# The first norm of a hybrid encoder step: x fetched transposed, with the factor per token spread by a matmul of ones

## The chip, the cores and the metric

The kernel runs on one core of a Trainium2 chip. A time is device microseconds (us) of one execution; the time of a kernel is the median of its runs. The engines are TensorE (PE, whose weight loads are listed apart as PEld), VectorE (DVE), ScalarE (ACT), GpSimd (POOL) and SyncE (SP, which here only issues DMAs).

## The reference, cut to what matters

One layer of an encoder runs over 2048 prompt tokens and 128 sample tokens. What the change touches is the first line: the norm of x and the projection behind it.

```python
def rms_norm(x, g):
    xf = x.astype(jnp.float32)
    y = xf * lax.rsqrt(jnp.mean(xf * xf, axis=-1, keepdims=True) + EPS)
    return (y * g.astype(jnp.float32)).astype(x.dtype)

h = rms_norm(x, norm_g[0])          # x: tokens x 1024
z = h @ w_in                        # 1024 x 3592, columns split among head groups
# band attention (8 heads), mLSTM (4 heads), w_out, residual,
# then the gated FFN with a causal convolution of width 3, residual
```

## The kernel before

**Work and stages.** The 2176 tokens are 17 tiles of 128: tiles 0 to 15 of the prompt and tile 16, the sample (SAMPLE in the code). They go in two halves, each in chunks of three tiles: [0 1 2] [3 4 5] [6 7 16], then [8 9 10] [11 12 13] [14 15]. For each half the kernel runs 14 weight groups of w_in in a fixed order, va0, qk0, qk1, va1 and so on; every matmul product is made of three (helper `mm3`, L105 to L107), of a high and a low float32r part of each operand. PE needs the model dimension on the partitions, so that the normed rows of a tile, tokens on the partitions, have to be turned: eight 128x128 blocks for each tile, 136 in all.

**One tile of the norm** (`norm_tile`, called by `norm_steps`). SP fetches the tile's 512 KB of rows into `xr` (L225). ACT squares it with a sum per row (L229). POOL makes mean and power -0.5 (L88, L94). DVE multiplies rows by the factor and by norm's row g, which one DMA has spread over all partitions (L232, L99). PE turns the eight blocks into one PSUM tile of two banks, `hT_pt` (L77). ACT rounds that to the high part (L211), DVE subtracts for the low part (L212). The chunk tile `hT` that results is what the projections of all 14 groups read.

**Buffers.** `xr` has no buffer of its own: tiles 0, 3, 6 and 8 to 15 take one of two buffers of the tag "xr", tiles 1, 4, 7 and 16 that of attention's "pth", tiles 2 and 5 that of "ptl" (`xr_tag`). A tile's fetch therefore waits until an earlier tile has let its buffer go. PSUM tiles of the tag "big" have two buffers, shared with attention's scores. A weight group arrives in two raw halves (`wi_raw`, L1231, one buffer after another from a pool with one buffer), each split by ACT and DVE (L1237, L1238) into the high and low part.

**Order.** The kernel is written as generators whose steps are interleaved by estimated costs: `pump` advances the attention and mLSTM pipelines while their DVE cost lags 0.615 of the PE cost. The framework's scheduler then sets the order of each engine's own queue; each engine, and SP's DMA queue, works its queue strictly in that order and waits at the head of it. In the first half no attention is under way during group va0, so that its nine tiles of norm and its projections stand alone at the start; in the second half the norm of tiles 8 to 15 lies beside the last group of the first half and va0 of the second. At the start SP also carries the chain of the attention bias (`reln`, `ext`, `relrow`, `nb`).

Of the kernel before, what the change touches and what calls it, by code (L numbers as in the profile page):

```python
# [10 lines left out]
F32 = mybir.dt.float32  # L11
F32R = mybir.dt.float32r
AF = mybir.ActivationFunctionType
ALU = mybir.AluOpType
# [3 lines left out]
P = 128  # L18
# [32 lines left out]
def hymba_step(ctx: ExitStack, tc: tile.TileContext, I: dict, O: dict):  # L51
# [38 lines left out]
    def rsqrt_mean(ssq, n, name, eps=EPS):  # L90
        ms = small.tile([P, 1], F32, tag="ms", name=name + "_ms")
        mean_square(ms, ssq, n, eps)
        rs = small.tile([P, 1], F32, tag="rs", name=name + "_rs")
        nc.gpsimd.tensor_tensor(rs, ms, nhalf[:, 0:1], op=ALU.pow)  # L94
# [127 lines left out]
    def norm_tile(t, chunk, j, bank):  # L222
        tag = xr_tag(t)
        xr = rows_tile(tag, [P, D], f"xr{t}")
        nc.sync.dma_start(xr, x_src(t))  # L225
        if not g0:
            g0.append(norm_row(0))
        ssq = small.tile([P, 1], F32, tag="ssq", name=f"ssq{t}")
        nc.scalar.activation(chunk[:, 0, :, j * P:(j + 1) * P], xr.rearrange("p (k c) -> p k c", k=KT), AF.Square,  # L229
                             accum_out=ssq)  # L230
        rs = rsqrt_mean(ssq, D, f"n0_{t}")
        nc.vector.scalar_tensor_tensor(xr, xr, rs, g0[0], op0=ALU.mult, op1=ALU.mult)  # L232
        rows_to_T(xr, chunk, j, f"hT{t}", bank)

    def evac_scaled(out, in_, scale):
        if scale is None:
# [1006 lines left out]
    def norm_steps(half):  # L1243

        for ci, tiles in enumerate(HALVES[half]):
            ch = phT.tile([P, 2, KT, 384], F32R, tag="hT", name=f"hT{half}_{ci}", bufs=3)
            chunks.append(ch)
            for j, t in enumerate(tiles):
                norm_tile(t, ch, j, ps_big)
                yield 0.9, 2.5  # L1250

    seq = [(half, gi) for half in range(2) for gi in range(14)]
    g0 = []
    pipes += [Pipe(att_stream()), Pipe(mem_stream())]
    chunks = []
    norms = norm_steps(0)
# [2 lines left out]
    for _ in pend[2]:  # L1259
        pass  # L1260
    next(norms)
    load_bias()
    for n_, (half, gi) in enumerate(seq):
        wh, wl, _ = pend
        split = iter([])
        if n_ + 1 < len(seq):
            pend = load_group(seq[n_ + 1][1])
            split = pend[2]
        g = GROUPS[gi]
        i = int(g[2])  # L1270
        nm = f"{g}_{half}"
        if g[:2] == "va":
            it = group_rows(wh, wl, half, chunks, vd[i], nm, 264 if gi == 0 else 256,
                            [O["v_prompt"][i], O["v_sample"][i].unsqueeze(1)])
        elif g[:2] == "qk":
            it = group_T(wh, wl, half, chunks, [qTd[i], kTd[i]], [-(DA ** -0.5), None], nm,
                         [None, [O["k_prompt"][i], O["k_sample"][i]]])
        elif g[:2] == "qb":
            it = group_T(wh, wl, half, chunks, [[t_[:, c, :] for t_ in qkbd[i]] for c in range(2)],
                         [None, DH ** -0.5], nm)  # L1280
        else:
            it = group_rows(wh, wl, half, chunks, vobd[i], nm)
        if half == 0 and gi == 13:
            chunks = []
            norms = norm_steps(1)
        if n_ == len(seq) - 1:
# [621 lines left out]
def lay_inputs(inp):  # L1908
    import numpy as np

    c = np.ascontiguousarray
    w_in = inp["w_in"][0].reshape(KT, P, 3592).transpose(1, 0, 2)
    va = [w_in[:, :, 1024 + 256 * i:1280 + 256 * i] for i in range(2)]
    gt = w_in[:, :, 3584:3592]
    qk = [np.concatenate([w_in[:, :, P * i:P * i + P], w_in[:, :, 512 + P * i:640 + P * i]], 2) for i in range(4)]
    qb = [np.concatenate([w_in[:, :, 1536 + P * i:1664 + P * i], w_in[:, :, 2048 + P * i:2176 + P * i]], 2)
          for i in range(4)]
    vo = [np.concatenate([w_in[:, :, 2560 + P * i:2688 + P * i], w_in[:, :, 3072 + P * i:3200 + P * i]], 2)
          for i in range(4)]
# [7 lines left out]
    out = {  # L1927
        "x_prompt": inp["x_prompt"][0],
        "x_sample": inp["x_sample"].reshape(P, D),
        "norm_g": inp["norm_g"][0],  # L1930
        "g_att": inp["g_att"].reshape(4, P).transpose(1, 0),
        "g_mlstm": inp["g_mlstm"],
        "w_in0": np.concatenate([va[0], gt], 2).reshape(P, 2112),
        "w_in1": np.stack(rest).reshape(13, P, 2048),
        "b_gate": np.concatenate([inp["b_i"], inp["b_f"]], 1),
        "rel_rev": inp["rel_table"][0][:, ::-1],
        "w_out": inp["w_out"][0].reshape(KT, P, D).transpose(1, 0, 2).reshape(P, KT * D),
        "w_up": w_up.reshape(NF, P, 2048),
        "w_conv": wc.reshape(4, 44, P).transpose(2, 1, 0),
        "w_down": np.stack([w_dn[:, :, i, j] for i, j in ((0, 0), (0, 1), (1, 1), (1, 0))], 2).reshape(NK, P, 2048),  # L1940
        "cache_k": inp["cache_k_att"][0].reshape(DB, 4, 2, 512, DA).transpose(0, 1, 2, 4, 3).reshape(DB, 4, P, 512),
        "cache_v": inp["cache_v_att"][0].reshape(DB, HA, 4, P, DA).transpose(0, 3, 2, 1, 4).reshape(DB, P, 4, 512),
        "cache_conv": inp["cache_ffn_conv"][0].reshape(DB, 2, 44, P).transpose(3, 2, 0, 1),
        "state_c": np.concatenate([inp["state_mlstm_n"][0][..., None], inp["state_mlstm_c"][0]], 3).transpose(1, 2, 0, 3),
        "state_m": inp["state_mlstm_m"][0].transpose(1, 0),
    }
    return {k: c(v) for k, v in out.items()}
# [51 lines left out]
```

## Time and profile before

| what | value |
|---|---|
| median of three runs | 2747.54 us (2746.0 to 2754.83) |
| span of the profiled execution, first to last instruction | 2745.7 us |
| the median above this span | 1.8 us |
| PE busy | 97% of the span |
| DVE, ACT, POOL busy | 70%, 53%, 26% |
| DMA, mean over the span | 203 GB/s |

The profile is of one execution; the time around its span is the 1.8 us of the table when it is set against the median. Busy shares are means over stages with different limits: the first 60 us and the FFN that fills the second half have little in common, so a stage is read by its own window.

### The profile page before, as it was taken

The numbers are of one execution on the slowest core, as the hardware profiler recorded it, in microseconds if no ns is written. First come the engines' busy times: TensorE is split into PE (matmuls) and PEld (weight loads), VectorE is DVE, ScalarE is ACT, GpSimd is POOL, SyncE is SP. The second block draws the span as 40 slices with busy tenths as digits, with TensorE's granted clock in tenths as the row PEclk, the third lists the DMA queues.
The fourth block names the chain that finished last, engine by engine and source line by source line (L and its number), as shares of the span: only waits on it lengthen the run. The fifth ranks groups of instructions, "written<-read, shape, count | busy, mean of one in ns | idle before, by whom it ended". The sixth has DMA issues, their size and how long they took to land.

```text
span 2745.7 us, 47826 instructions
## 1 busy us (share of the span) xinstructions
PE 2672.3 (97%) x16323; PEld 2500.7 (91%) x16323; DVE 1922.9 (70%) x3643; ACT 1456.3 (53%) x2961; POOL 708.5 (26%) x1373
## 2 busy tenths in 40 slices
PE   7999999999999999999999999999999999999998
PEld 7899999998899998877899997789999888999976
DVE  5345445646546667756899998758888876899956
ACT  4355545635346666634445556654554665555554
POOL 1000010212100002335455542023333212565401
PEclk9999999999999999999999999999999999999999
DMA  5544355546564557668887668767886777798875
GB/s 184 159 118 139 106 156 166 170 151 206 156 192 125 154 157 225 195 213 287 300 244 229 219 203 271 246 198 200 223 221 189 230 252 239 212 246 240 254 260 184
DMA packets 335635, 557.03 MB, mean 203 GB/s; under 512 B 61890, under 2 KB 168222, under 8 KB 335070
## 3 DMA queue, kind: packets, MB, share of 16 engines
q1 hardware_dynamic: 253230, 406.60, 48.1%
q0 software_dynamic: 43568, 113.54, 14.3%
q10 hardware_dynamic: 38592, 33.83, 3.7%
q8 instruction: 128, 2.10, 0.3%
q14 instruction: 117, 0.96, 0.1%
HBM read 389.77 MB, written 173.49 MB: 205 GB/s over the span
## 4 chain that ended last, share of the span: by engine, by line
PE 42%; DVE 5%; DMA 3%; issue 1%; ACT 1%; POOL 0%; DVEq 0%; SPq 0%; POOLq 0%; ACTq 0%
PE uec L105 5%; PE uec L106 5%; PE uec L107 5%; PE dn L107 3%; PE dn L105 3%; PE dn L106 3%; PE ua L107 3%; PE ua L105 3%; PE ua L106 3%; PE ub L107 1%; PE ub L106 1%; PE ub L105 1%; PE dnm L107 1%; PE dnm L106 1%; PE dnm L105 1%
## 5 line engine op out<-in xcount | busy, mean ns | idle before, releaser
L105 PE MATMUL uec<-B,wuh 128*128 128x384 f32 (+1 forms) x720 | 236.0, 328 | 6.0 <-DVE ug L1498 3.8
L106 PE MATMUL uec<-B,wuh 128*128 128x384 f32 (+1 forms) x720 | 235.1, 327 | 0.0
L107 PE MATMUL uec<-B,wul 128*128 128x384 f32 (+1 forms) x720 | 234.4, 327 | 0.0
L1327 ACT CAST wuh<-wu 128x512 fp32r<-128x512 f32 x255 | 141.7, 618 | 110.9 <-PE uec L106 107.7
L1328 DVE TENSOR_TENSOR al<-ar,ah 128x768 fp32r<-128x768 f32 (+2 forms) x141 | 108.7, 780 | 117.4 <-ACT ah L1327 117.1
L107 PE MATMUL dn<-wdh,al 128*128 128x512 f32 x462 | 186.1, 403 | 3.6 <-DVE al L1328 3.6
L105 PE MATMUL dn<-wdh,ah 128*128 128x512 f32 x462 | 183.5, 397 | 4.6 <-ACT ah L1327 2.9
L106 PE MATMUL dn<-wdl,ah 128*128 128x512 f32 x462 | 182.6, 395 | 0.0
L1327 ACT CAST ah<-ar 128x768 fp32r<-128x768 f32 (+2 forms) x141 | 96.1, 692 | 151.3 <-PE dnm L106 113.3
L1328 DVE TENSOR_TENSOR wul<-wu,wuh 128x512 fp32r<-128x512 f32 x255 | 164.7, 686 | 2.4 <-ACT wuh L1327 2.4
L406 DVE CUSTOM_DVE_ANT_0 tmp<-s,nb 128x640 f32<-128x640 f32 (+4 forms) x128 | 94.4, 738 | 92.8 <-PE s L396 92.1
L105 PE MATMUL vo<-wi_h,hT 128*128 128x256 f32 x544 | 155.6, 286 | 0.6 <-DVE mt L212 0.6
L107 PE MATMUL vo<-wi_h,hT 128*128 128x256 f32 x544 | 155.9, 287 | 0.0
L106 PE MATMUL vo<-wi_l,hT 128*128 128x256 f32 x544 | 155.1, 285 | 0.0
L1328 DVE TENSOR_TENSOR wdl<-wdr,wdh 128x512 fp32r<-128x512 f32 x231 | 145.5, 686 | 8.0 <-ACT wdh L1327 5.9
L105 PEld LDWEIGHTS uec<-B,wuh 128*128 128x128 f32 x720 | 135.1, 188 | 9.1 <-issue 4.7
L106 PEld LDWEIGHTS uec<-B,wuh 128*128 128x128 f32 x720 | 135.3, 188 | 0.2
L105 PE MATMUL qk<-hT,wi_h 128*128 128x384 f32 (+1 forms) x384 | 129.1, 336 | 6.2 <-ACT qk_st L237 4.7
L107 PEld LDWEIGHTS uec<-B,wul 128*128 128x128 f32 x720 | 135.1, 188 | 0.0
L419 DVE TENSOR_TENSOR ptl<-pt,pth 128x640 fp32r<-128x640 f32 (+4 forms) x128 | 93.6, 738 | 57.9 <-ACT pth L418 57.0
L1327 ACT CAST wdh<-wdr 128x512 fp32r<-128x512 f32 x231 | 127.2, 620 | 11.6 <-PE uec L106 7.4
L407 ACT ACTIVATE tmp<-tmp,mn 128x640 f32<-128x640 f32 (+4 forms) x128 | 97.6, 763 | 64.7 <-DVE mn L406 61.9
(425 smaller groups left out, 9201.7 us busy)
## 6 DMA issues: line engine op xcount, KB each, us to landing
wu<-in_w_up SPq DMA_DIRECT2D x220, 256.0 KB, 4.4
wu<-wsd SPq DMA_DIRECT2D x176, 256.0 KB, 5.3
wdr<-wtd SPq DMA_DIRECT2D x132, 256.0 KB, 4.6
wi_raw<-in_w_in SPq DMA_DIRECT2D x52, 512.0 KB, 4.1
wdr<-in_w_down SPq DMA_DIRECT2D x99, 256.0 KB, 4.9
wsd<-ws POOLq DMA_DIRECT2D x88, 256.0 KB, 5.1
ar<-ad_S SPq DMA_DIRECT2D x50, 384.0 KB, 5.2
kraw<-kTd SPq DMA_DIRECT2D x112, 128.0 KB, 3.5
```

The lines of the kernel that those rows point to most:

```text
L105: nc.tensor.matmul(out, ah, bh, start=start, stop=False, skip_group_check=onto)
L106: nc.tensor.matmul(out, ah, bl, start=False, stop=False, skip_group_check=onto)
L107: nc.tensor.matmul(out, al, bh, start=False, stop=stop, skip_group_check=onto)
L406: nc.vector.tensor_tensor_reduce(o_, s_, b_, 1.0, 3e38, ALU.add, ALU.min, accum_out=mn)
L407: nc.scalar.activation(tmp[:, :n], tmp[:, :n], AF.Exp, bias=mn, scale=-1.0, accum_out=rsum[:, i % 4, hh:hh + 1])
L419: nc.vector.tensor_tensor(s.ptl[:, sl, qc], ptv, s.pth[:, sl, qc], op=ALU.subtract)
L1327: nc.scalar.copy(h, r)
L1328: nc.vector.tensor_tensor(l, r, h, op=ALU.subtract)
```

## The change

Each tile of x is now fetched twice. `x_T` is laid out by the host as the transposed tile, 1024 values on each of 128 partitions, partition by model dimension within a block of 128. `norm_factor` fetches the rows as before (`xq`), but only for the sum of squares; its power of -0.5 is written to one column of `nrs`. For tiles 0 to 7 and 16 it is called within the tile's step, for tiles 8 to 15 during groups 1 to 4 of the first half. `norm_tile` then works on the transposed tile `xt`: POOL multiplies it by g, which is now a column of eight values per partition (`g0`), spread along the tokens; POOL scales the identity by the tile's factors (`diag`); PE multiplies a matrix of ones by that, in float32, so that each partition of PSUM holds the 128 factors as a row; DVE multiplies `xt` by that row; ACT rounds and DVE subtracts, both from SBUF now. The steps announce 0.2 in place of 0.9 of PE cost to `pump`.

```diff
-        xr = rows_tile(tag, [P, D], f"xr{t}")
+    def norm_factor(t):
+        xr = rows_tile("xr", [P, D], f"xq{t}") if 8 <= t < SAMPLE else pa.tile(
+            [P, D], F32, tag=("kh", "kl")[t % 2], name=f"xq{t}", bufs=2)
         nc.sync.dma_start(xr, x_src(t))
-        if not g0:
-            g0.append(norm_row(0))
-        nc.scalar.activation(chunk[:, 0, :, j * P:(j + 1) * P], xr.rearrange("p (k c) -> p k c", k=KT), AF.Square,
-                             accum_out=ssq)
-        rs = rsqrt_mean(ssq, D, f"n0_{t}")
-        nc.vector.scalar_tensor_tensor(xr, xr, rs, g0[0], op0=ALU.mult, op1=ALU.mult)
-        rows_to_T(xr, chunk, j, f"hT{t}", bank)
+        nc.scalar.activation(xr, xr, AF.Square, accum_out=ssq)
+        mean_square(ms, ssq, D)
+        nc.gpsimd.tensor_tensor(nrs[:, t:t + 1], ms, nhalf[:, 0:1], op=ALU.pow)
+    def norm_tile(t, chunk, j):
+        xt = rows_tile(xr_tag(t), [P, D], f"xt{t}")
+        nc.sync.dma_start(xt, I["x_T"][t])
+        if not 8 <= t < SAMPLE:
+            norm_factor(t)
+        nc.gpsimd.tensor_tensor(xt, xt, g0.unsqueeze(2).broadcast_to([P, KT, P]), op=ALU.mult)
+        diag = pa.tile([P, 256], F32, tag="sh", name=f"diag{t}", bufs=1)[:, :P]
+        nc.gpsimd.tensor_scalar(diag, ident, nrs[:, t:t + 1], None, op0=ALU.mult)
+        row = ps_big(f"hT{t}_rs")[:, :P]
+        nc.tensor.matmul(row, ones, diag, start=True, stop=True)
+        nc.vector.tensor_tensor(xt, xt, row.unsqueeze(1).broadcast_to([P, KT, P]), op=ALU.mult)
+        nc.scalar.copy(chunk[:, 0, :, cols], xt)
+        nc.vector.tensor_tensor(chunk[:, 1, :, cols], xt, chunk[:, 0, :, cols], op=ALU.subtract)
...
-                norm_tile(t, ch, j, ps_big)
-                yield 0.9, 2.5
+                norm_tile(t, ch, j)
+                yield 0.2, 2.5
...
+            if half == 0 and 1 <= gi <= 4 and u % 6 == 3:
+                for t in [next(factors, None)]:
+                    if t is not None:
+                        norm_factor(t)
```

Three places of the queues bear on what follows. The first is SP's queue at the start, up to the second half of the first weight group, `wi0_raw1`; `xr`, `xt` and `xq` are the tiles of x with their numbers. Before, from the queue's first fetch:

```order
L225 DMA xr0_319<-in_x_prompt 128x1024
L99 DMA norm_row0_321<-in_norm_g 128x1024
L1231 DMA wi0_raw0_343<-in_w_in0 128x1056
L225 DMA xr1_355<-in_x_prompt 128x1024
L302 DMA reln_375<-in_rel_rev 8x384
L225 DMA xr2_394<-in_x_prompt 128x1024
L225 DMA xr3_446<-in_x_prompt 128x1024
L1304 DMA bgate_306<-in_b_gate 128x8
L1305 DMA gatt_317<-in_g_att 128x4
L616 DMA mss_885<-in_state_m 4x8
L504 DMA hgm0_0_4058<-in_g_mlstm 128x128
L1231 DMA wi0_raw1_349<-in_w_in0 128x1056
```

After, behind the queue's first seven fetches (g0, xt0, xq0, wi0_raw0, xt1, xq1, reln):

```order
L241 DMA xt2_391<-in_x_T 128x1024
L231 DMA xq2_393<-in_x_prompt 128x1024
L241 DMA xt3_440<-in_x_T 128x1024
L231 DMA xq3_442<-in_x_prompt 128x1024
L1329 DMA bgate_310<-in_b_gate 128x8
L231 DMA xq4_492<-in_x_prompt 128x1024
L1330 DMA gatt_321<-in_g_att 128x4
L636 DMA mss_913<-in_state_m 4x8
L524 DMA hgm0_0_4049<-in_g_mlstm 128x128
L99 DMA norm_row1_13054<-in_norm_g 128x1024
L1251 DMA wi0_raw1_349<-in_w_in0 128x1056
```

Of fetches of 512 KB and more, `wi0_raw1` was the seventh and is now the twelfth.

The second is the same queue further on, where the sample tile 16 is fetched, the last tile of the first half. Before, from the fourth fetch behind `wi0_raw1` on:

```order
L225 DMA xr4_499<-in_x_prompt 128x1024
L1231 DMA wi1_raw0_392<-in_w_in1 128x1024
L225 DMA xr5_550<-in_x_prompt 128x1024
L225 DMA xr7_651<-in_x_prompt 128x1024
L1231 DMA wi1_raw1_497<-in_w_in1 128x1024
L225 DMA xr8_6702<-in_x_prompt 128x1024
L1231 DMA wi2_raw0_812<-in_w_in1 128x1024
L225 DMA xr16_700<-in_x_sample 128x1024
```

After, behind `wi0_raw1`, ext, xq5, ext, xt6, xq6, xq7, xq16, xt4, relrow, xt5, wi1_raw0, xq8 and nb0 (in this order):

```order
L241 DMA xt7_633<-in_x_T 128x1024
L231 DMA xq9_1008<-in_x_prompt 128x1024
L335 DMA relrow_302<-ext_955 128x767
L335 DMA relrow_302<-ext_955 128x767
L1251 DMA wi1_raw1_488<-in_w_in1 128x1024
L231 DMA xq10_1184<-in_x_prompt 128x1024
L335 DMA relrow_302<-ext_955 128x767
L231 DMA xq11_1286<-in_x_prompt 128x1024
L358 DMA nb1_0_1366<-relrow_302 128x640
L241 DMA xt16_679<-in_x_T 128x1024
```

The transposed sample tile now stands behind the rows of tiles 9 to 11, the second half of the next weight group and four of the eight bias fetches, which stood behind it before. The buffer of xq9 is that of xt6, the buffer of xt7 that of xt4.

The third is POOL's queue for tiles 3 to 7 and 16. Before, it held two small instructions for each tile:

```order
L88 TENSOR_SCALAR n0_3_ms_450<-ssq3_448 128x1
L94 TENSOR_TENSOR n0_3_rs_452<-n0_3_ms_450,nhalf_77 128x1
L88 TENSOR_SCALAR n0_4_ms_503<-ssq4_501 128x1
L94 TENSOR_TENSOR n0_4_rs_505<-n0_4_ms_503,nhalf_77 128x1
L88 TENSOR_SCALAR n0_5_ms_554<-ssq5_552 128x1
L94 TENSOR_TENSOR n0_5_rs_556<-n0_5_ms_554,nhalf_77 128x1
```

After, from the product of tile 6 on:

```order
L245 TENSOR_TENSOR xt6_587<-xt6_587,g0_298 128x1024
L247 TENSOR_SCALAR diag5_548<-ident_72,nrs_299 128x128
L88 TENSOR_SCALAR n0_6_ms_593<-ssq6_591 128x1
L236 TENSOR_TENSOR nrs_299<-n0_6_ms_593,nhalf_77 128x1
L247 TENSOR_SCALAR diag6_597<-ident_72,nrs_299 128x128
L88 TENSOR_SCALAR n0_7_ms_639<-ssq7_637 128x1
L236 TENSOR_TENSOR nrs_299<-n0_7_ms_639,nhalf_77 128x1
L88 TENSOR_SCALAR n0_16_ms_685<-ssq16_683 128x1
L245 TENSOR_TENSOR xt4_490<-xt4_490,g0_298 128x1024
L236 TENSOR_TENSOR nrs_299<-n0_16_ms_685,nhalf_77 128x1
L245 TENSOR_TENSOR xt5_538<-xt5_538,g0_298 128x1024
L247 TENSOR_SCALAR diag7_643<-ident_72,nrs_299 128x128
```

A product of 128x1024 and a scaled identity have come in for each tile, and the products of tiles 4 and 5 stand behind that of tile 6 and behind the factors of tiles 6, 7 and 16.

More of the change, by code (lines that the diff above doesn't have):

```diff
@@ L220, in rows_tile @@
         return pa.tile(shape, dtype, tag=tag, name=name, bufs=1)
-    def norm_tile(t, chunk, j, bank):
-        tag = xr_tag(t)
-        xr = rows_tile(tag, [P, D], f"xr{t}")
+    g0 = const.tile([P, KT], F32, name="g0")
+    nrs = const.tile([P, 17], F32, name="nrs")
+    ones = pa.tile([P, P], F32, tag="ones", name="ones", bufs=1)
+    nc.vector.memset(ones, 1.0)
+    def norm_factor(t):
+        xr = rows_tile("xr", [P, D], f"xq{t}") if 8 <= t < SAMPLE else pa.tile(
+            [P, D], F32, tag=("kh", "kl")[t % 2], name=f"xq{t}", bufs=2)
         nc.sync.dma_start(xr, x_src(t))
-        if not g0:
-            g0.append(norm_row(0))
         ssq = small.tile([P, 1], F32, tag="ssq", name=f"ssq{t}")
-        nc.scalar.activation(chunk[:, 0, :, j * P:(j + 1) * P], xr.rearrange("p (k c) -> p k c", k=KT), AF.Square,
-                             accum_out=ssq)
-        rs = rsqrt_mean(ssq, D, f"n0_{t}")
-        nc.vector.scalar_tensor_tensor(xr, xr, rs, g0[0], op0=ALU.mult, op1=ALU.mult)
-        rows_to_T(xr, chunk, j, f"hT{t}", bank)
+        nc.scalar.activation(xr, xr, AF.Square, accum_out=ssq)
+        ms = small.tile([P, 1], F32, tag="ms", name=f"n0_{t}_ms")
+        mean_square(ms, ssq, D)
[3 more added lines that the diff above has]
+        nc.sync.dma_start(xt, I["x_T"][t])
+        xt = xt.rearrange("p (k n) -> p k n", k=KT)
+        if not 8 <= t < SAMPLE:
[6 more added lines that the diff above has]
+        nc.vector.tensor_tensor(xt, xt, row.unsqueeze(1).broadcast_to([P, KT, P]), op=ALU.mult)
+        cols = slice(j * P, (j + 1) * P)
+        nc.scalar.copy(chunk[:, 0, :, cols], xt)
+        nc.vector.tensor_tensor(chunk[:, 1, :, cols], xt, chunk[:, 0, :, cols], op=ALU.subtract)
     def evac_scaled(out, in_, scale):
@@ L1248, in norm_steps @@
             for j, t in enumerate(tiles):
-                norm_tile(t, ch, j, ps_big)
-                yield 0.9, 2.5
+                norm_tile(t, ch, j)
+                yield 0.2, 2.5
     seq = [(half, gi) for half in range(2) for gi in range(14)]
-    g0 = []
+    nc.sync.dma_start(g0, I["g_in"])
     pipes += [Pipe(att_stream()), Pipe(mem_stream())]
@@ L1261, in hymba_step @@
     next(norms)
+    factors = iter(range(8, 16))
     load_bias()
@@ L1929, in lay_inputs @@
         "x_sample": inp["x_sample"].reshape(P, D),
+        "x_T": np.concatenate([inp["x_prompt"][0], inp["x_sample"].reshape(P, D)]).reshape(17, P, KT, P)
+            .transpose(0, 3, 2, 1).reshape(17, P, D),
         "norm_g": inp["norm_g"][0],
+        "g_in": inp["norm_g"][0, 0].reshape(KT, P).transpose(1, 0),
         "g_att": inp["g_att"].reshape(4, P).transpose(1, 0),
```

## The prediction

> **What bounds the kernel now.** I read the page first (busy shares, slices, the chain that ended last), then what PE waited for, then the windows of the stages that hold the norm. The page's lines are the span, the busy times, PE and DMA by fortieths of the span, and the chain.
>
> ```profile
> span 2745.7 us, 47826 instructions
> PE 2672.3 (97%) x16323; PEld 2500.7 (91%) x16323; DVE 1922.9 (70%) x3643; ACT 1456.3 (53%) x2961; POOL 708.5 (26%) x1373
> PE   7999999999999999999999999999999999999998
> DMA  5544355546564557668887668767886777798875
> PE 42%; DVE 5%; DMA 3%; issue 1%; ACT 1%; POOL 0%; DVEq 0%; SPq 0%; POOLq 0%; ACTq 0%
> ```
>
> PE is busy nearly everywhere, so a PE instruction less is time less, except where PE already waits. Only the first slice falls to 7, and that is where nine of the 17 tiles of the norm lie. The view of who waited for whom, for PE (total, times, longest):
>
> ```profile
> PE hT_pt L77 <- DVE xr L232: 10.1, 4, 8.2
> PE qk L105 <- ACT qk_st L237: 4.7, 2, 3.5
> PE va L105 <- ACT hT L211: 2.8, 2, 1.7
> ```
>
> The longest wait is the 8.2 us before the first transpose. The windows hold busy time (and instructions) of each engine, then PE's granted clock, the DMA share and rate:
>
> ```profile
> 2.00:14.00 12.00, 3.54 (x14) 2.84 (x15) 5.32 (x7) 6.52 (x12) 2.88 (x10) 1.00 0.95 326
> 14.00:42.00 28.00, 27.60 (x220) 27.27 (x218) 20.72 (x28) 16.28 (x27) 4.68 (x10) 1.00 0.57 188
> 42.00:56.00 14.00, 11.43 (x81) 10.90 (x80) 2.92 (x5) 3.02 (x7) 0.74 (x2) 1.00 0.09 29
> 56.00:100.00 44.00, 41.56 (x235) 39.00 (x235) 19.79 (x80) 14.14 (x34) 0.58 (x4) 1.00 0.59 177
> 110.00:114.00 4.00, 4.00 (x18) 4.00 (x18) 0.43 (x2) 1.09 (x4) 0.77 (x2) 0.66 0.32 100
> 525.00:550.00 25.00, 22.63 (x184) 21.46 (x183) 19.12 (x46) 17.77 (x41) 5.84 (x13) 1.00 0.71 223
> 550.00:575.00 25.00, 22.83 (x158) 21.53 (x157) 15.03 (x58) 7.85 (x24) 4.78 (x18) 1.00 0.46 138
> ```
>
> From 2 to 14 us the DMA engines are full (0.95 of them, 0.326 MB a us): the start is bound by fetches. From 14 to 42 PE is full, from 42 to 56 it waits 2.6 us. In the second half's norm (around 508 to 550) PE loses 2.4 us of 25.
>
> **What goes, what comes.** Groups of instructions by shape, with the mean ns of one, and one tile's eight weight loads in the timeline:
>
> ```profile
> L77 PE MATMUL hT_pt<-ident,xr 128*128 128x128 f32 x136 | 20.0, 292 | 10.5 <-DVE xr L232 10.1 <-DVE gates L286 0.4
> L699 PE MATMUL ms<-mqk 128*128 128x128 f32 x128 | 25.1, 278 | 3.1 <-DVE num L717 1.3 <-DVE w L705 1.1 <-DMA mqk<-qkbd 0.7
> 20.88 0.90 PEld L77 LDWEIGHTS hT_pt<-ident,xr 128*128 128x128 f32 x8
> L232 DVE SCALAR_TENSOR_TENSOR xr<-xr,n_rs,norm_row 128x1024 f32<-128x1024 f32 x17 | 21.9, 1292 | 16.0 <-POOL n_rs L94 10.2 <-DMA norm_row<-in_norm_g 5.3 <-POOL mvo L685 0.5
> L212 DVE TENSOR_TENSOR hT<-hT_pt,hT 128x1024 fp32r<-128x1024 f32 x17 | 20.7, 1220 | 3.8 <-ACT hT L211 3.7
> L229 ACT ACTIVATE hT<-xr 128x1024 fp32r<-128x1024 f32 x17 | 18.0, 1059 | 14.2 <-DMA xr<-in_x_prompt 9.8 <-DMA xr<-in_x_sample 4.2
> L211 ACT CAST hT<-hT_pt 128x1024 fp32r<-128x1024 f32 x17 | 17.1, 1008 | 2.5 <-PE hT_pt L77 1.9 <-ACT va_st L237 0.4
> ```
>
> PE loses 17 times 0.90 us of transposes, 15.3 us. It gains 17 float32 matmuls of 128 columns: at least a transpose's share (0.90/8 = 0.11 us), at most the 0.28 of L699; I take 0.19, 3.2 us. DVE and ACT keep the same count of 128x1024 passes, at 1.2 and 1.0 us. POOL gains a two-input pass of 128x1024 and a scaled identity for each tile, of which the trace shows none. Its nearest rows:
>
> ```profile
> L686 POOL TENSOR_SCALAR_AFFINE_SELECT mb<-mb 128x256 f32<-128x256 f32 x32 | 16.0, 502 | 168.7 <-DMA mb<-md 128.8 <-ACT kw L704 14.9 <-ACT jk L655 11.7
> masks.py:199 POOL TENSOR_SCALAR_AFFINE_SELECT ident<-ident 128x128 f32<-128x128 f32 x1 | 0.3, 283 | 0.1
> L94 POOL TENSOR_TENSOR n_rs<-n_ms,nhalf 128x1 f32<-128x1 f32 x56 | 35.6, 636 | 4.4
> ```
>
> From 128 to 256 columns the one-input select grows by 0.22 us, so 1024 columns are 1.8 us; with two inputs, up to twice that, 3.5. I take 2.4, nearer the select, because that is a measured pass of the same engine and type and the doubling is only assumed. The scaled identity is a one-input pass of 128 columns, 0.3. The Trainium skill speaks against the place of this pass: "GPSIMD Engine Reference", section 3, "Performance versus the Vector engine", calls this engine the wrong choice for plain elementwise arithmetic and gives 4497 ns for a two-input add of 2048 float32 columns. An estimate by that page is 2.2 us for 1024 columns, and the sum would come out 0.2 us lower at each pass that is waited for; no run here shows the pass yet.
>
> POOL and DVE also get in each other's way in this trace. A power of 128x2 on POOL, alone and started inside a DVE pass with two SBUF inputs:
>
> ```profile
> 553.41 0.70 POOL L660 TENSOR_TENSOR mf<-ad,nhalf 128x2 f32<-128x2 f32 x1
> 539.29 1.28 DVE L232 SCALAR_TENSOR_TENSOR xr<-xr,n_rs,norm_row 128x1024 f32<-128x1024 f32 x1 [2.20 <-POOL n_rs L94]
> 539.51 1.62 POOL L660 TENSOR_TENSOR mf<-ad,nhalf 128x2 f32<-128x2 f32 x1
> ```
>
> The second power lasted to 541.13, 0.56 after the DVE pass ended at 540.57: it waited the pass out and then ran. "SBUF — State Buffer", section "Who interferes with whom", in the Trainium skill states this as a lock: a DVE instruction with two SBUF inputs and a GpSimd instruction that reads SBUF exclude each other, and whichever comes first keeps the ports to its end; this trace agrees (0.56 us behind the pass). With the change the low-part subtraction has both inputs in SBUF, where one was PSUM, and POOL's passes are 2.4 us long.
>
> **The start, step by step.** Issues in the first 70 us (KB each, us to landing), then the moments that matter: the weight half that lets va0 run on, the sample tile's issue and landing, and the copy that ends its projection.
>
> ```profile
> xr<-in_x_prompt SPq DMA_DIRECT2D x9, 512.0 KB, 3.7
> relrow<-ext SPq DMA_DIRECT2D x6, 383.5 KB
> nb<-relrow SPq DMA_DIRECT2D x2, 320.0 KB
> 14.40 1.17 ACT L1237 CAST wi_h<-wi_raw 128x528 fp32r<-128x528 f32 x2 [0.48 <-DMA wi_raw<-in_w_in]
> 36.32 0.33 SPq L225 DMA_DIRECT2D xr<-in_x_sample  x1
> 41.58 1.06 ACT L229 ACTIVATE hT<-xr 128x1024 fp32r<-128x1024 f32 x1 [4.24 <-DMA xr<-in_x_sample]
> 55.73 0.37 ACT L237 COPY va_st<-va 128x256 f32<-128x256 f32 x1 [7.41 <-PE va L107]
> 18.55 0.19 PEld L105 LDWEIGHTS va<-wi_h,hT 128*128 128x128 f32 x1
> 18.68 0.19 PEld L106 LDWEIGHTS va<-wi_l,hT 128*128 128x128 f32 x1
> 94.76 0.34 PE L105 MATMUL qk<-hT,wi_h 128*128 128x384 f32 x1
> 95.28 0.33 PE L105 MATMUL qk<-hT,wi_h 128*128 128x384 f32 x1
> ```
>
> At 0.326 MB a us, 512 KB (0.524 MB) take 1.6 us, a bias fetch 1.2, nb 1.0. The weight half moves from seventh to twelfth: 5 x 1.6 = 8 us later, at 22.5. Five more tiles precede xt4, so it lands at 22.5 + 6 x 1.6 = 32.1; POOL, DVE, ACT, DVE (2.4 + 1.2 + 1.0 + 1.2, and 0.5 of handing over) free its buffer at 38.4, and xt7 lands 3.7 later, at 42.1. DVE still has the products of tiles 5 and 6, two weight splits of 0.7 and two subtractions: 6.2 us, so tile 6's buffer is free at 44.6, or at 47 if POOL's product of tile 7 (42.1 to 44.5) shuts the subtractions out. Only then can SP issue xq9, and behind it wait two relrow, wi1_raw1, xq10, relrow, xq11, nb1 and xt16: five of 1.6, three of 1.2, one of 1.0, and 2 us to get going, 14.7. The sample tile lands at 59 to 62. POOL, DVE and ACT add 5.1, and PE then has 24 matmuls of 0.12 and 23 of 0.17 (0.52 for three in the last two rows), 6.9 us: 71 to 74, in place of 55.7, so 15 to 18 us late. PE stands idle over 5 us more than once on the way, and after the 3.5 us idle of the second wait quoted above its clock was 0.66 for 4 us: 1.4 us more. A queue of this length has waits that I haven't counted, so I take 19. The bounds: if SP never waits at the head, 14 tiles and weight halves, four relrow, two nb and the tile itself put xt16 at 22.5 + 22.4 + 4.8 + 2 + 1.6 = 53.3 and the end at 65.3, 10 us late; with passes of 3.5 and a fetch rate a fifth lower, 30. The nine tiles' transposes, 8.1 us, bring nothing here, because PE waits longer than that.
>
> **The second half's norm.** Eight tiles save 7.2 us of transposes and pay 1.5 for the matmuls. The fetch of a tile waits for the buffer of the one two before. Before, a buffer was held for the fetch 3.7, square 1.2, POOL 0.7, DVE 1.3 and transposes 1.0, 7.9 us; now 3.7, POOL 2.4, DVE 1.2, ACT 1.0, DVE 1.2, 9.5. With two buffers that is 0.8 us a tile, over tiles 10 to 15 about 4.8, if nothing else covers it; nothing if attention and mLSTM do, 9 if the lock adds as much again. Net -1 (-6 to +3). Squares of tiles 8 to 15 move to the first 80 us, on ACT at a time when it waits.
>
> **The sum.** 2745.7 + 19 - 1 = 2763.7 for the span, and 1.8 from span to median: 2766. Between 56 and 125 us, where PE idles some 6 us, I set nothing, with 4 either way.
>
> **Rivals.** A measurement of this kernel can tell about 0.3%, 8.2 us, from no change.
> First, faster: the x fetches find room. DMA is used 0.57 from 14 to 42 and 0.09 from 42 to 56, room for some 8 MB; if queue order costs nothing, PE's 15.3 - 3.2 = 12 us come back and the time is 2735. It decides so if xt16 lands before about 44, so that tile 16 is ready when PE comes to it, near 48. Against it: 53 is the earliest that I can make of the bytes. Chance 0.08.
> Second, no change: SP hardly waits (10 us late), the second half keeps its 6, and bias and rows fetched early shorten the waits between 56 and 125: 2747.5 + 10 - 6 - 2 = 2750. Chance 0.12.
> Third, slower still: the lock decides. If every one of 17 subtractions meets a POOL pass halfway, 17 x 1.2 = 20 us are lost on DVE, and half of them on the path: 2766 + 10 = 2776; DVE and POOL would then have no idle time in 14 to 70 and 510 to 560. The change's own norm is then slower than the transposes it removes. Chance 0.12.
> The forecast, fetches and queue order at the start, has 0.68.
>
> **Numbers.** The forecast gives 2766. Its bounds, 10 to 30 at the start and -6 to +3 later with 4 either way, span 2748 to 2784; I give 2750 to 2784, which leaves out the first rival and the far ends. Slower holds the forecast and the third rival, 0.80; the second is the same, 0.12; the first is faster, 0.08.
>
> **What would show it.** In the profile after: the first slice of PE at 6 or below in place of 7, the DMA share from 14 to 42 well above 0.57; the cast of wi0_raw1 near 22; SP's issue of xq9 at 44 or later; ACT's copy of tile 16's va between 70 and 80; POOL's 128x1024 pass near 2.4 us; PE's work less by about 12 us. The forecast is wrong if tile 16's copy comes before 60, or if the loss at the start is there but given back before 130, or if the second half's norm adds over 5.

## The result, and the profile after

The changed kernel takes 2790.5 us (median of 4 runs, 2782.7 to 2792.0), the kernel before 2751.2 (4 runs): ratio 1.0144, 95% interval 1.0122 to 1.0165, some 39 us slower. The forecast was slower, 2766 (2750 to 2784): the sign is right, the loss is twice as large, and the time lies 6.5 us above the range. The profiled execution of after is its fastest, 2782.7 us with a span of 2780.9, so the two traces differ by 35.2 us.

The page of after: span, busy times, PE, granted clock and DMA by fortieths, chain.

```profile
span 2780.9 us, 47693 instructions
PE 2686.8 (97%) x16221; PEld 2510.5 (90%) x16221; DVE 1932.5 (69%) x3644; ACT 1458.6 (52%) x2961; POOL 753.9 (27%) x1407
PE   6999999999999999999999999999999999999998
PEclk9999999999999999999999999999999999999999
DMA  7534445456564556658877768766877677688775
PE 41%; DVE 6%; DMA 4%; issue 2%; ACT 1%; POOL 0%; DVEq 0%; POOLq 0%; SPq 0%; ACTq 0%
```

The page looks almost as it did: in the first slice PE falls from 7 to 6 and DMA rises from 5 to 7. PE has 102 instructions less, yet is busy 14.5 us longer. Its granted clock is lower in places: by the trace's record of the clock, the time lost to it ((1 - clock) x duration, summed over the span) is 27 us in after and 9 in before, so that up to 17 of the 35 us lie in slower instructions. The groups of the new norm (mean ns of one, then the idle time before them), and what PE waited for:

```profile
L249 PE MATMUL hT_rs<-diag,ones 128*128 128x128 f32 x34 | 9.9, 381 | 22.5 <-POOL diag L247 15.3 <-DVE xt L250 4.5 <-POOL mvo L705 2.7
L245 POOL TENSOR_TENSOR xt<-xt,g 128x1024 f32<-128x1024 f32 x17 | 33.8, 1988 | 26.9 <-PE spt L77 15.1 <-DMA xt<-in_x_T 8.7 <-DVE num L737 1.9
L247 POOL TENSOR_SCALAR diag<-ident,nrs 128x128 f32<-128x128 f32 x17 | 16.3, 960 | 11.5 <-DVE attT L458 6.0 <-PE hT_rs L249 5.0
L250 DVE TENSOR_TENSOR xt<-xt,hT_rs 128x1024 f32<-128x1024 f32 x17 | 20.5, 1213 | 11.8 <-POOL xt L245 7.0 <-PE hT_rs L249 4.8
L253 DVE TENSOR_TENSOR hT<-xt,hT 128x1024 fp32r<-128x1024 f32 x17 | 25.4, 1496 | 4.4 <-ACT hT L252 4.4
```

```profile
PE hT_rs L249 <- POOL diag L247: 15.3, 5, 11.1
PE va L105 <- ACT hT L252: 7.1, 3, 4.1
PE cus L814 <- DMA cs<-in_state_c: 5.8, 4, 3.2
PE hT_rs L249 <- DVE xt L250: 4.5, 5, 3.1
PE va L107 <- DVE hT L253: 4.1, 4, 1.8
```

A row matmul stands in the trace as two records and keeps PE busy for 9.9 / 17 = 0.58 us, where the eight transposes of a tile took 20.0 / 17 = 1.18 by the same count. Windows of the two norms, in the columns of the prediction:

```profile
2.00:14.00 12.00, 0.80 (x2) 0.50 (x2) 3.15 (x5) 4.38 (x8) 7.58 (x12) 1.00 0.96 365
14.00:42.00 28.00, 19.10 (x110) 17.33 (x110) 18.09 (x17) 17.68 (x31) 23.79 (x31) 0.99 0.80 296
42.00:56.00 14.00, 13.47 (x90) 13.47 (x91) 8.78 (x12) 6.70 (x12) 5.21 (x8) 0.78 0.93 328
525.00:550.00 25.00, 19.88 (x144) 18.27 (x142) 19.24 (x37) 12.84 (x33) 11.55 (x14) 0.93 0.50 153
550.00:575.00 25.00, 19.62 (x123) 17.83 (x123) 20.27 (x37) 9.35 (x21) 15.46 (x25) 0.84 0.61 187
575.00:600.00 25.00, 24.01 (x153) 23.69 (x154) 16.14 (x61) 8.54 (x26) 2.38 (x9) 0.89 0.58 177
```

From 14 to 42 us PE runs 110 matmuls where it ran 220 (54 of them transposes), and POOL is the busiest engine. In the second half's norm PE idles 5 us in each of two windows where it idled 2.3, and the granted clock falls to 0.93, 0.84 and 0.89, where the two windows shown of before had 1.00; (1 - clock) x 25 us, summed, is another 8.5 us.

Where the 35 us come from shows when the two traces are laid side by side at the same instructions. The copy that ends tile 16's va0, and the one that ends va0 of the second half (before: 55.73, in the prediction, and the last row here):

```profile
70.09 0.37 ACT L257 COPY va_st<-va 128x256 f32<-128x256 f32 x1 [0.55 <-PE va L107]
584.89 0.37 ACT L257 COPY va_st<-va 128x256 f32<-128x256 f32 x1 [2.91 <-PE va L107]
```
```profile
561.20 0.37 ACT L237 COPY va_st<-va 128x256 f32<-128x256 f32 x1 [1.36 <-PE va L107]
```

In the same way for other points, this is how much later than before each stands (us). The columns to the right belong to kernels of the experiments.

| point (its time in before) | after | own_diag | credit_09 | own_diag_credit | before_put_off |
|---|---|---|---|---|---|
| copy of tile 16's va0 (55.7) | +14.4 | +20.6 | +18.8 | +21.9 | +6.2 |
| last copy of qb3, first half (480.0) | +8.5 | +16.1 | +15.9 | +20.7 | +4.0 |
| last copy of va0, second half (561.2) | +23.7 | +23.1 | +28.1 | +18.4 | +6.0 |
| last copy of vo1, second half (893.8) | +14.8 | +11.2 | +19.9 | +22.4 | +7.2 |
| first wo on PE (1053.7) | +8.2 | +13.9 | +20.6 | +14.9 | -0.8 |
| last wo (1326.1) | +30.0 | +15.5 | +20.3 | +35.4 | +22.1 |
| last dn (2736.7) | +35.3 | +20.4 | +28.4 | +41.2 | +28.1 |

So after loses 14 at the start and keeps 8.5 of it; 15 more come in the second half's norm, of which 6 are left at vo1; and 22 come between the first and the last wo, in a stage in which the change has no instruction. That last loss was in no term of the forecast. PE's order shows what lies in that stage: the matmuls of attention and mLSTM that stand ahead of the first wo number 1710 in before and 1673 in after. The planner pays attention work out by the credits of the steps; with the norm step's credit at 0.2 in place of 0.9, and the norm's instructions standing elsewhere, 37 of these matmuls have moved behind the first wo. The stage between the first and the last wo, one window each, of after, then of before:

```profile
1061.90:1356.10 294.20, 277.06 (x1473) 231.51 (x1472) 197.22 (x371) 140.96 (x340) 113.10 (x215) 0.98 0.70 232
```
```profile
1053.70:1326.10 272.40, 263.46 (x1414) 219.74 (x1413) 183.35 (x339) 129.24 (x312) 113.98 (x206) 1.00 0.74 240
```

The stage is 21.8 us longer: PE is busy 13.6 longer with 59 more records, some 5 of it by the lower clock (0.98), and idles 8.2 more.

### The profile page after: what moved, and what is told of

It is laid out like the page before. It is cut to its first block, busy times and chain, and to the rows that moved or that the text cites. A ratio compares the mean times of both kernels' runs of the same rounds, so it can differ in the third digit from the quotient of the medians.

```text
span 2780.9 us, 47693 instructions
## 1 busy us (share of the span) xinstructions
PE 2686.8 (97%) x16221; PEld 2510.5 (90%) x16221; DVE 1932.5 (69%) x3644; ACT 1458.6 (52%) x2961; POOL 753.9 (27%) x1407
## 3 DMA queue, kind: packets, MB, share of 16 engines
q0 software_dynamic: 43568, 113.54, 13.9%
## 4 chain that ended last, share of the span: by engine, by line
PE 41%; DVE 6%; DMA 4%; issue 2%; ACT 1%; POOL 0%; DVEq 0%; POOLq 0%; SPq 0%; ACTq 0%
PE uec L105 5%; PE uec L106 5%; PE uec L107 5%; PE dn L107 3%; PE dn L105 3%; PE dn L106 3%; PE ua L107 2%; PE ua L105 2%; PE ua L106 2%; PE dnm L107 1%; PE dnm L106 1%; PE dnm L105 1%; PE ub L107 1%; PE ub L105 1%; PE ub L106 1%
## 5 line engine op out<-in xcount | busy, mean ns | idle before, releaser
L1258 DVE TENSOR_TENSOR wi_l<-wi_raw,wi_h 128x512 fp32r<-128x512 f32 (+1 forms) x112 | 75.4, 704 | 78.2 <-ACT wi_h L1257 77.8
```

Of the source, the lines that this page charges most:

```text
L1258: nc.vector.tensor_tensor(l[:, c], r, h[:, c], op=ALU.subtract)
```

## Experiments

Three theories went in. A: the scaled identity takes the buffer of attention's tile "sh"; tile 8's waits for attention, and the second half's norm starts late. B: what costs is attention put off until after the first wo. C, the forecast's: the loss is made in the first 70 us.

**own_diag, credit_09, own_diag_credit**: the buffer, the credit, both.

```diff
# own_diag
-        diag = pa.tile([P, 256], F32, tag="sh", name=f"diag{t}", bufs=1)[:, :P]
+        diag = diags[:, (t % 8) * P:(t % 8 + 1) * P]
# credit_09
-                yield 0.2, 2.5
+                yield 0.9, 2.5
```

> The scaled identity gets a buffer that attention does not use. Tile 8's row matmul then stands 260 matmuls behind the first of vo3 in PE's order, where it stood 317 behind (the first transpose of before: 223), and 1712 matmuls of attention and mLSTM stand ahead of the first wo, where 1673 stood (before: 1710). Theory A, the second half's norm starts late because the scaled identity waits for attention's buffer: the gates copy of tile 15, 23.7 us later than before in the changed kernel, comes about 10 later, and 12 us of the total come back: 2778. Theory B, what costs is attention that was put off until after the first wo: 18 us come back, 2772. Both together: 2762. Theory C, the forecast's, all of the loss is made in the first 70 us: no change, 2790.

> Only the credit that the planner gives a norm step, 0.9 in place of 0.2. The scaled identity still uses attention's buffer (row matmul of tile 8 at 280 matmuls into vo3), but 1709 matmuls of attention and mLSTM stand ahead of the first wo, as before. Theory A (late scaled identity): at most 4 us, 2786 to 2790. Theory B (attention put off): the lag between the first and the last wo, 22 us in the changed kernel, goes: about 2772. Theory C (first 70 us alone): 2790.

> Both edits. The row matmul of tile 8 stands 221 matmuls into vo3, as early as the transposes did, but only 1669 matmuls of attention and mLSTM stand ahead of the first wo: more is put off than in the changed kernel. Theory A: 2776 to 2778. Theory B: 2790. Theory C: 2790.

Measured, against before in the same runs: own_diag 1.0072 (1.0055 to 1.0090), credit_09 1.0096 (1.0078 to 1.0113), own_diag_credit 1.0158 (1.0138 to 1.0178): about 20, 26 and 43 us. The two that keep 1712 and 1709 matmuls ahead of the first wo win 20 and 13 us over after; the one that keeps 1669 wins nothing, though its scaled identity never waits for attention. C alone is out, and B carries most. The same stage in own_diag is as long as in before, with as many records:

```profile
1067.60:1341.60 274.00, 264.36 (x1414) 220.25 (x1412) 181.93 (x337) 128.83 (x311) 111.61 (x204) 1.00 0.72 238
```

In the table own_diag and credit_09 are nearly level from the first wo to the last (+1.6 and -0.3), after and own_diag_credit fall back by 21.8 and 20.5. Against that stand the 9.4 that after wins in the three groups ahead of the first wo (from +17.6 at qb2 to +8.2): the work put off is missing there. The net is 12.

**before_put_off**: the kernel before, transposes and all, with the credit alone changed so that 1668 matmuls stand ahead of the first wo.

```diff
-                yield 0.9, 2.5
+                yield 0.4, 2.5
```

> The kernel before, with its transposes; only the planner's credit of a norm step is 0.4 in place of 0.9. 1668 matmuls of attention and mLSTM then stand ahead of the first wo, where 1710 stood. Theory B (attention that is put off until after the first wo costs 15 us, the gap between the two pairs of kernels that differ in it): 2766, and the lag against before rises by about 20 between the first and the last wo. Theories A (late scaled identity) and C (first 70 us alone): 2751, since no operation of the norm is touched.

Measured: 1.0076 (1.0057 to 1.0096), about 21 us, with no operation of the norm touched. The table has it level with before at the first wo and 22.1 late at the last, and its stage has the numbers of after:

```profile
1052.90:1348.20 295.30, 277.31 (x1474) 231.49 (x1473) 196.02 (x370) 140.90 (x340) 112.83 (x215) 0.98 0.71 230
```

B holds. Some 5 us of its loss are made at the start instead, by the order that the credit gives there.

**new_first_half, second_half_only**: each half's norm alone; the other half keeps its transposes.

```diff
-                norm_tile(t, ch, j)
-                yield 0.2, 2.5
+                if half == 0:           # second_half_only: half == 1
+                    norm_tile(t, ch, j)
+                    yield 0.2, 2.5
+                else:
+                    norm_tile_old(t, ch, j, ps_big)
+                    yield 0.9, 2.5
...
-    factors = iter(range(8, 16))        # new_first_half
+    factors = iter([])
...
-            if half == 0 and 1 <= gi <= 4 and u % 6 == 3:   # second_half_only
+            if half == 0 and 6 <= gi <= 9 and u % 6 == 3:
```

> The new norm for tiles 0 to 7 and 16 only; tiles 8 to 15 go through the old one, with no early fetch of their rows. 1711 matmuls stand ahead of the first wo, so nothing is put off. The forecast's start (SP's queue with the rows of tiles 8 to 11 in it, 19) minus those four fetches of 1.6 and the wait at the first of them: tile 16's copy 8 to 10 us late and 2760. If those fetches cost nothing and the chain of each tile (POOL, PE, DVE, ACT, DVE) is what is late: tile 16's copy 15 to 20 late and 2768.

> The other half alone: the old norm for tiles 0 to 7 and 16, the new one for 8 to 15, whose factors are made in groups 6 to 9 of the first half, away from the start. The scaled identity keeps attention's buffer; 1709 matmuls stand ahead of the first wo. The forecast's term for the second half, -1: 2750. Theory A (the scaled identity waits and tiles 8 to 15 come late): 5 to 10 more, 2756 to 2761.

Measured: 1.0042 (1.0026 to 1.0057) and 1.0043 (1.0030 to 1.0055), 12 us each. new_first_half ends tile 16's copy 10.9 late, stays 5 to 10 late after that and ends 11.0 late, so the start alone costs some 11. second_half_only is 2 us ahead of before when vo3 of the first half ends, 14.8 late at the end of va0 and 10 to 11 late from there to the first wo. (At the end it is 19 late: its trace is of the slowest of its 12 executions.) Its norm costs 12 by the medians, where the forecast had -1.

**own_diag_late**: own_diag with the factors of tiles 8 to 15 made in groups 6 to 9, so that their fetches leave the start.

```diff
-            if half == 0 and 1 <= gi <= 4 and u % 6 == 3:
+            if half == 0 and 6 <= gi <= 9 and u % 6 == 3:
```

> The changed kernel with the scaled identity's own buffer (2769), and the factors of tiles 8 to 15 made in groups 6 to 9 in place of 1 to 4, so that eight fetches leave the first 80 us; 1712 matmuls stand ahead of the first wo. If the fetches ahead of xt16 in SP's queue make the start late: tile 16's copy 8 us earlier than in that kernel and 2761. If not: 2769.

Measured: 1.0075 (1.0060 to 1.0089), no gain over own_diag. Tile 16's copy, of own_diag and of this kernel:

```profile
76.34 0.37 ACT L258 COPY va_st<-va 128x256 f32<-128x256 f32 x1 [7.50 <-PE va L107]
```
```profile
73.10 0.35 ACT L258 COPY va_st<-va 128x256 f32<-128x256 f32 x1
```

So tile 16 comes 3.2 us earlier without these fetches, not 8, and the total gains nothing (between after and new_first_half, which has none of them either, it is 14.4 less 10.9, 3.5). Even the 3.2 can't be put down to the fetches: up to these two copies the lower clock took 8.5 us in own_diag and 5.2 here.

**no_product**: own_diag without GpSimd's product; the gain g of the first norm is left out.

```diff
-        nc.gpsimd.tensor_tensor(xt, xt, g0.unsqueeze(2).broadcast_to([P, KT, P]), op=ALU.mult)
```

> The kernel own_diag (2769) without GpSimd's product with g, so the gain of the first norm is left out; 1711 matmuls of attention and mLSTM stand ahead of the first wo. If GpSimd's pass (1.9 us) lies in the chain of every tile of the start, tile 16's copy comes 5 to 8 us earlier and the total is 2762 to 2764. If fetches alone bound the start, nothing changes: 2769. If the pass also holds up DVE's subtractions (one of them lasted 2.9 us in place of 1.2), a few us more come back in the second half: 2758.

Measured: 1.0027 (1.0016 to 1.0038), 12 us under own_diag, and tile 16's copy 14.5 earlier than there (3.4 of it by the clock, which took 5.1 us up to here):

```profile
61.80 0.35 ACT L257 COPY va_st<-va 128x256 f32<-128x256 f32 x1
```

Fetches alone don't bound the start: the pass is on its path, with more than any expectation gave it. From the second half's norm on it runs 6 us ahead of before, PE's saving at last, but only 2.5 are left at the last wo, and 7 are lost behind it.

**g_on_dve**: own_diag with both products on DVE, block by block.

```diff
-        nc.gpsimd.tensor_tensor(xt, xt, g0.unsqueeze(2).broadcast_to([P, KT, P]), op=ALU.mult)
...
-        nc.vector.tensor_tensor(xt, xt, row.unsqueeze(1).broadcast_to([P, KT, P]), op=ALU.mult)
+        for k in range(KT):
+            nc.vector.scalar_tensor_tensor(xt[:, k, :], xt[:, k, :], g0[:, k:k + 1], row, op0=ALU.mult, op1=ALU.mult)
```

> The kernel own_diag (2769) with GpSimd's product gone and g kept: DVE makes both products, as eight instructions of 128x128 per tile, (x times g of that block) times the factors' row, in place of one of 128x1024 (1.2 us). 1711 matmuls of attention and mLSTM stand ahead of the first wo. If GpSimd's pass is what made the start late (no_product 2756): 2756 to 2760, the few us for eight short passes, and tile 16's copy 6 to 9 us after before's. If any extra time in the chain of a tile costs as much, wherever it runs: 2763 to 2769.

Measured: 1.0089 (1.0073 to 1.0106), no better than own_diag. The group of its DVE in the first 80 us says why:

```profile
L251 DVE SCALAR_TENSOR_TENSOR xt<-xt,g,hT_rs 128x128 f32<-128x128 f32 x72 | 19.4, 341 | 4.4 <-DMA xt<-in_x_T 2.2 <-PE hT_rs L249 2.1
```

Eight of 0.34 are 2.7 us in place of 1.9 on POOL and 1.2 on DVE. The chain of a tile is shorter by 0.4, DVE carries 1.5 more, and tile 16's copy comes at 72.15, 4.2 before own_diag's. That fits time in a tile's chain as the cost, wherever it runs, and not POOL alone; the run doesn't tell a longer chain from a fuller DVE, since both grow by 1.5 a tile over no_product.

**second_half_own_s600, before_s600, before_s630**: other shares of the planner (0.600 and 0.630 for 0.615), to have own_diag's buffer in the second half without work put off, and to put work off by other means.

```diff
-    SHARE = 0.615
+    SHARE = 0.600       # before_s630: 0.630
```

> The old norm for tiles 0 to 7 and 16, the new one for 8 to 15 with the scaled identity in its own buffer and late factors; the planner's share is 0.600 in place of 0.615 so that 1706 matmuls stand ahead of the first wo (with 0.615 it would be 1669). Theory A (what made second_half_only 13 us slower than before is that the scaled identity waits for attention's buffer): at most 3 us from its control, the kernel before at that share. If the new norm itself makes tiles 8 to 15 late: 8 to 13 above the control.

> The control: the kernel before with the planner's share at 0.600 in place of 0.615; 1716 matmuls of attention and mLSTM stand ahead of the first wo (1710 at 0.615). Theory B: the same as before within 4 us, 2747 to 2751, since nothing more is put off.

> The kernel before with the planner's share at 0.630, credit unchanged: 1671 matmuls of attention and mLSTM stand ahead of the first wo (1710 at 0.615). Theory B, if it is the work put off and not the credit of the norm steps that costs: 15 to 24 above before, 2764 to 2772, with 1474 matmul records between the first and the last wo where before had 1414. Otherwise: 2748 to 2752.

Measured: 1.0119 (1.0105 to 1.0133), 1.0043 (1.0031 to 1.0056) and 1.0055 (1.0043 to 1.0068). The first pair decides nothing: the control is itself 12 us slower, with 1716 matmuls ahead of the first wo, so that number is not the whole of what the planner's order costs. (In before_s600 the last score of attention ends 32 us late though the count is full, and 6.5 are lost at the start.) before_s630 is 15 slower, with the 1474 records in the stage that B expected, but the stage gains only 11.4 and another 8 are lost in va0 of the second half. B's size is thus 6 to 14 net of what is won ahead of the first wo, by kernel; its sign is the same in each.

**g_on_dve_second_half and its twin**: the old norm for tiles 0 to 7 and 16, the new one for 8 to 15 with g on DVE and late factors; the scaled identity in its own buffer or in attention's. Planner untouched, 1711 matmuls ahead of the first wo in both.

```diff
-                norm_tile(t, ch, j)
-                yield 0.2, 2.5
+                if half == 1:
+                    norm_tile(t, ch, j)        # with g_on_dve's products
+                    yield 0.2, 2.5
+                else:
+                    norm_tile_old(t, ch, j, ps_big)
+                    yield 0.9, 2.5
...
+        diag = diags[0][:, (t % 8) * P:(t % 8 + 1) * P]   # shared: the tile "sh", as in after
```

> The old norm for tiles 0 to 7 and 16 (so a start as before), the new one for 8 to 15 with the product on DVE, the scaled identity in its own buffer, factors in groups 6 to 9; planner untouched, 1711 matmuls stand ahead of the first wo. With the start, the put-off work, the shared buffer and GpSimd's pass all gone, what is left is PE's gain, 8 tiles at 0.90 less 0.58, and up to 5 us that no_product gained over own_diag in the second half: 2742 to 2748. If the new norm makes tiles 8 to 15 late for another reason: 2755 to 2761.

> The same, but the scaled identity in attention's buffer: tile 8's row matmul stands 273 matmuls into vo3 where it stood 210, and again 1711 stand ahead of the first wo. Theory A (the shared buffer makes tiles 8 to 15 late): 6 to 9 us above its twin. Otherwise the same as its twin within 3.

Measured: 0.9989 (0.9979 to 0.9999) and 1.0026 (1.0015 to 1.0038): the buffer alone, with the later place that it gives the row matmul in PE's order, is worth 10 us, a little more than A asked for, and the twin that has its own is, by 3 us, the only kernel here that beats before. When tile 10's fetch could be issued, in before, in after (a row of two holds two fetches, the first at its start; the rows behind it are the next pairs'), then in the twins, own buffer first:

```profile
510.33 2.56 SPq L225 DMA_DIRECT2D xr<-in_x_prompt  x2
```
```profile
537.16 3.58 SPq L241 DMA_DIRECT2D xt<-in_x_T  x2
549.90 1.87 SPq L241 DMA_DIRECT2D xt<-in_x_T  x2
561.69 0.47 SPq L241 DMA_DIRECT2D xt<-in_x_T  x1
```
```profile
514.88 0.33 SPq L242 DMA_DIRECT2D xt<-in_x_T  x1
```
```profile
527.45 0.35 SPq L241 DMA_DIRECT2D xt<-in_x_T  x1
```

At the end of qb3, ahead of this, the twins stand 1.6 and 5.0 later than before, so of the 12.6 us between their fetches some 9 are the buffer's. In after it is POOL's scaled identity of tile 8 that waits, and nothing of the tile can go on without it:

```profile
528.15 0.61 POOL L247 TENSOR_SCALAR diag<-ident,nrs 128x128 f32<-128x128 f32 x1 [6.01 <-DVE attT L458]
```

## Where the prediction held and where it failed

**The start, 19.** Measured 14.4 at tile 16's copy, which the working itself put at 15 to 18, and 8.5 that last; new_first_half has 11 in the total. The size is right to within its bounds at that copy, but the path that the working described is not the one that the trace shows. ACT's cast of wi0_raw1, predicted for 22.5:

```profile
23.81 1.16 ACT L1257 CAST wi_h<-wi_raw 128x528 fp32r<-128x528 f32 x2
```

Then, in order, xt4's issue, its product on POOL and on DVE, xt7's issue, xq9's (predicted for 44.6 to 47), the subtractions of tiles 5 and 6, that of tile 7, and xt16's issue:

```profile
23.99 0.33 SPq L241 DMA_DIRECT2D xt<-in_x_T  x1
33.70 1.90 POOL L245 TENSOR_TENSOR xt<-xt,g 128x1024 f32<-128x1024 f32 x1
35.63 1.22 DVE L250 TENSOR_TENSOR xt<-xt,hT_rs 128x1024 f32<-128x1024 f32 x1 [4.77 <-POOL xt L245]
39.24 0.33 SPq L241 DMA_DIRECT2D xt<-in_x_T  x1
40.05 0.33 SPq L231 DMA_DIRECT2D xq<-in_x_prompt  x1
42.85 4.04 DVE L253 TENSOR_TENSOR hT<-xt,hT 128x1024 fp32r<-128x1024 f32 x2
49.14 1.23 DVE L253 TENSOR_TENSOR hT<-xt,hT 128x1024 fp32r<-128x1024 f32 x1 [1.11 <-ACT hT L252]
50.39 0.33 SPq L241 DMA_DIRECT2D xt<-in_x_T  x1
```

The step that failed here is "Only then can SP issue xq9, and behind it wait" the fetches up to xt16. xq9 left before the subtraction of tile 6 had begun, so it didn't wait for that tile's buffer, which the text ahead of the prediction also gives it; it left as ACT's square of xq8 ended (40.03). And xt16 left 0.02 us after tile 7's subtraction: it waited for tile 7's buffer, not for the fetches ahead of it. So it is in own_diag_late and new_first_half too (0.03 us behind that subtraction in both), which have no rows of tiles 8 to 15 there. Tiles 1, 4, 7 and 16 hand on one buffer. Their fetches left at 2.19, 15.24, 24.41 and 36.32 before and at 2.65, 23.99, 39.24 and 50.39 after, so the delay is made at the first two handovers, 8.3 and 6.1 us. Of the second, 5.0 us are a wait in POOL's queue: xt4 had landed at 28.7, and POOL was busy until 33.70 with work that stands ahead of its product, the scaled identities of tiles 5 and 6 and the factors of tiles 6, 7 and 16 among it. The working had no such wait. That it has tile 4's buffer free at 38.4, close to 39.24, is luck: the fetch had landed 3.4 earlier than it said.

This is why the rows of tiles 8 to 15, to which the working gave 4.8 of its 14.7 us ahead of xt16, and the wait at the first of them, were worth 3 at most (own_diag_late), while GpSimd's pass was worth 14.5 (no_product). A shorter chain frees a tile's buffer sooner, and the next fetch with it, at each of three handovers; the working charged the pass at one of them, or two.

**The small prices.** POOL's 128x1024 pass takes 2.0 us on average, 1.9 where it runs freely, against 2.4 taken. The 2.2 estimated by section 3 of "GPSIMD Engine Reference" in the Trainium skill was nearer. The scaled identity takes 0.6 us at best, not 0.3, and 0.96 on average. The row matmul takes 0.58 of PE, not 0.19, so PE's saving by its own count was 20.0 - 9.9 = 10 and not 12.

**The lock (third rival, 20 us on DVE).** It is there, but smaller. A DVE subtraction and the POOL product it ran into:

```profile
27.40 2.92 DVE L253 TENSOR_TENSOR hT<-xt,hT 128x1024 fp32r<-128x1024 f32 x1
```
```profile
27.25 1.98 POOL L245 TENSOR_TENSOR xt<-xt,g 128x1024 f32<-128x1024 f32 x1
```

POOL's pass ends at 29.23 and the subtraction 1.1 us later, its own length of 1.2 as good as whole: it waited the pass out. "SBUF — State Buffer", "Who interferes with whom", in the Trainium skill says so, and the trace agrees. Over 17 tiles the subtractions average 1.50 in place of 1.22, 4.7 us in all. POOL pays too: eight of its 17 scaled identities take 0.8 us or more, each beside a DVE pass with two SBUF inputs, 6 us in all. That rival's 2776 came nearer the result than the forecast for another reason than its own.

**The second half's norm, -1.** This step failed: "Net -1 (-6 to +3)". The prediction's own sign for it, that this norm adds over 5, came true. The -1 holds for the kernel that has its own buffer and no POOL pass (2746, 3 under before); in after, the lag grows by 15 in that norm and 6 last, and alone it costs 12 (second_half_only). The step counted how long a tile's buffer is held, but not that the scaled identity had been given a buffer of attention's. Both of the cycles that it counted were too short, but their difference was about right: after's fetches of tiles 10, 12 and 14 follow each other by 12.7 and 11.8 us (537.16, 549.90, 561.69) for 9.5, before's by 10.6 and 11.0 (510.33, 520.97, 531.98) for 7.9, so 1.4 us apart on average for 1.6.

**What was left out.** The sum, "2745.7 + 19 - 1", holds nothing behind the second half's norm. That is the largest error in after: the credit went from 0.9 to 0.2, the planner put 37 matmuls of attention and mLSTM off, and between the first and the last wo 22 us are lost, some 12 net. Each cause alone costs 12 (new_first_half), 12 (second_half_only) and 21 (before_put_off, 5 of them at the start), together 45 for the 39 measured, so they don't add up exactly. The prediction walked through the norm's own instructions and took the rest of the order as given; the count ahead of the first wo could be read from the order without a run.

**What stays open.** Why own_diag is 6 us later than after at tile 16, when the shared buffer has no work of attention in it yet; the lower clock is 3.4 of it (8.5 us lost to it up to that copy, for 5.1), and the order that credits and shares give the start moves that point by 6 in the old norm also. What keeps tile 1's buffer 8.3 us longer was not taken apart. And the stages behind the last wo add 5 us in after, up to 12 in other kernels (own_diag_late) and under 1 in new_first_half; executions of one kernel lie up to 15 us apart (2765 to 2780 in before_put_off), so single traces don't settle it. How much of the clock's 17 us would go if the waits went was not tried.

## What to carry to other kernels

In a kernel whose order comes from a planner, a change of a step's cost is a change of everything that is ordered by it: compare the whole order, far from the edit, and count what has moved across each stage's border before pricing the edit itself. A helper buffer that is borrowed from another stage's pool of one is a wait on that stage, whatever its size. Where a start is bound by fetches into few buffers, each us added to the time for which a buffer is held is paid again at every handover (three here, from tile 1 to tile 16), so a pass on an engine with time to spare isn't free there. Ask of each late fetch which buffer it waits for before counting the fetches ahead of it.

## What the runs showed of the hardware

A 128x128 scalar-and-row product on DVE takes 0.34 us with its row in PSUM, so that eight cost 2.7 us where one product of 128x1024 takes 1.2. A float32 matmul of 128 columns that stands alone is two records and keeps PE busy for 0.58 us, about four times one of eight transposes in a row by the same count (1.18 / 8 = 0.15).

The granted clock took far more than the 1.4 us that the prediction gave it: 3.1 us from 42 to 56 us (0.78), and 8.5 in the second half's norm. In after's record of the clock it is at 1.00 or 0.50, the latter in stretches of 3.4, 6.8 or 10.2 us. In the 6.5 us before each of them PE had idled for 1.7 to 4.1 us. Around the first:

```profile
36.00:42.00 6.00, 1.86 (x14) 1.51 (x12) 4.89 (x5) 5.10 (x9) 5.26 (x8) 0.94 0.28 83
42.00:48.00 6.00, 5.47 (x25) 5.47 (x26) 6.00 (x7) 1.71 (x3) 4.19 (x4) 0.50 0.85 305
```

In these places a wait of PE is paid twice, once as idle time and once in the slower matmuls behind it.
